# A two-batch encoder layer: all input projections first, in pairs of column tiles with seven products over both batches, and the recurrence after them

## The chip, the cores and the metric

The kernel runs on one core of a Trainium2 chip. The metric is device time of one execution in microseconds: 1835.03 us is the median of two runs (1832.98 to 1837.08). The profiled execution took 1835.74 us. The engines are named as in the profile: PE (TensorE, with PEld for its weight loads), DVE (VectorE), ACT (ScalarE), POOL (GpSimd), SP (SyncE, which issues most transfers).

## What is computed

One layer is applied to two independent requests ("batches") of 512 tokens x 1024 with the same weights. Cut to its core:

```python
h = rmsnorm(x, norm_mix_g)
gates, p_a, pq, pkv, pkr = split(h @ w_in)          # 2048 | 1824 | 256 | 128 | 32 columns
p_a = token_shift(p_a, shift_mu)                    # p + mu0*(previous - p) + mu1*(next - p)
pr, pk, pv, pwf, pwb, paf, pab, pg = split(p_a)     # 3 x 512, 4 x 64, 160
w = exp(-exp(-softplus(-(w0 + tanh(pw) @ w2)) - 0.5))   # decay, forward and backward
a = sigmoid(a0 + pa @ a2);  g = sigmoid(pg) @ g2
# per head of 64, in both directions:
#   S = S*w - (S kk) (kk*a)^T + v k^T ;  o = S r
y_a = ((groupnorm(o_f + o_b) + bonus) * g) @ w_oa
y_b = attention(rmsnorm(pq) @ w_uq, rmsnorm(pkv) @ w_ukv, rope) @ w_ob
x = x + (sigmoid(g_A)*y_a + sigmoid(g_B)*y_b) @ w_out
x = x + (silu(h2 @ w_g) * (h2 @ w_u)) @ w_down ;  out = rmsnorm(x)      # h2 = rmsnorm(x)
```

Everything is float32. Large products are made from operands split into a high and a low part: `mm3` issues three matrix products (high x high, high x low, low x high) that are added in PSUM.

## The kernel before

*Projections.* x is normed and transposed (`norm_T`) into h_hi and h_lo, one pair of tiles per batch. The columns of w_in are cut into 35 tiles of 128. `proj` makes one tile for both batches: 8 steps of 128 rows x 3 products x 2 batches = 48 products of 512 columns (tile 4 in halves of 256). `lora_phase` makes the tiles w, a, g, x and, with `lu` and `lug`, the low-rank products behind them; it ends with the first head pair's r, k and v (`rkv_tiles(0)`). Then `latents` makes the three tiles of q and kv with their norms.

*The recurrence* is made in eight units, one per head pair p and batch b, in the order p outer, b inner. A unit has a preparation (norm of kk with the power on POOL, L714; the gx and gy products; the nt products sent through DRAM as nt_d; on POOL a loop of multiply and subtract over "lanes", L839 and L841, which inverts small triangular blocks), a merge (zp, xp), the state steps (`state`, 8 chunks of three dependent products s with copies between them) and a post part (group norm: mp, ss_gn, rbp_gn, bp) which writes y_d.

*The order of the work.* From the first unit on, `drive` interleaves generators: states, posts, merges and preparations have priority, and fill and combine come last. A planner's clock (`pe["now"]`, advanced by the cost of each product) decides which generator may go on; a yield names how long it is to be left alone. The program order that results is kept on PE (`keep_in_program_order`). The fill is: the other rkv tiles, 16 gate tiles (`gate_tile`), then attention. After the eighth unit `combine` runs per batch: loads of y_d and o_d (`ld`), for each of 8 column tiles j the products pab of both branches, their gates, and the operand m. It is followed by the projection pwo with w_out in quarters of 256 columns, the norm, and the FFN, which already makes its products with seven in place of eight (`gate_up`, `prod`).

*Queues.* SP issues its transfers in the order of its program; a transfer that waits for a semaphore holds those behind it. POOL likewise has one order of lanes, powers and additions.

## Time and profile before

| what | value |
|---|---|
| median of two runs | 1835.03 us |
| profiled execution: time, span | 1835.74 us, 1834.0 us |
| busy PE, DVE, ACT, POOL | 1734.3, 1116.9, 771.0, 642.2 us |
| first projection product, first gx of unit 0 | 27.8, 197.6 us |
| first scores of attention (sc), last state step (s) | 725.8, 898.6 us |
| first pab, first product of the FFN (pgA) | 945.9, 1159.6 us |

A row of the timeline or of the chain gives a start in us, a length and the instruction; x8 means eight of them in a row, and brackets hold the idle time before it with what ended it. A row of a window gives the stretch, its length and, for each engine, the busy time and the number of instructions. A row of groups gives line, engine, operation, out<-in, shapes and count, then busy us and the mean ns of one.

### The profile page before, as it was taken

What the parts mean: (1) busy time and instruction counts of PE and PEld (TensorE: products, weight loads), DVE (VectorE), ACT (ScalarE), POOL (GpSimd) and SP (SyncE); (2) the same over time, 40 slices, a digit from 0 to 9 for tenths busy, and PEclk for the clock granted to TensorE, in tenths of its full rate; (3) what the DMA queues carried; (4) which work ended last, traced back from release to release, by engine and by line L of the source; (5) the groups of instructions that cost most, each with busy time, mean ns of one, the idle gap of its engine ahead of it and who ended that gap; (6) DMA issues with size and microseconds to landing.
All of it is one profiled execution on the core that took longest, in us unless ns stands there. A gap on an engine that the chain in (4) does not pass through costs nothing.

```text
span 1834.0 us, 31000 instructions
## 1 busy us (share of the span) xinstructions
PE 1734.3 (95%) x11676; PEld 1365.7 (74%) x11676; DVE 1116.9 (61%) x1957; ACT 771.0 (42%) x1496; POOL 642.2 (35%) x992
## 2 busy tenths in 40 slices
PE   6999999999999998899989999699999999989997
...
GB/s 163 123 175 163 123 107 82 124 71 136 81 125 106 89 113 119 61 36 55 21 233 249 190 178 35 24 81 93 103 95 84 92 81 92 98 273 134 121 139 92
DMA packets 185333, 208.97 MB, mean 114 GB/s; under 512 B 102816, under 2 KB 114464, under 8 KB 185184
## 3 DMA queue, kind: packets, MB, share of 16 engines
...
q10 hardware_dynamic: 720, 0.98, 0.2%
q0 software_dynamic: 144, 0.52, 0.1%
q14 instruction: 57, 0.47, 0.1%
HBM read 147.70 MB, written 59.24 MB: 113 GB/s over the span
## 4 chain that ended last, share of the span: by engine, by line
PE 70%; DVE 9%; DMA 8%; POOL 5%; issue 3%; ACT 2%; SPq 1%; DVEq 0%; POOLq 0%; ACTq 0%
PE pgC L125 9%; PE pj_gt L125 8%; PE pgB L125 6%; PE pgA L125 6%; PE pj_rkv L125 5%; PE dx L125 5%; PE dy L125 3%; PE s L125 3%; PE pab L125 2%; PE sc L125 2%; PE pav L125 2%; PE pj_mla L125 2%; DMA wor<-in_w_out 2%; PE o L125 2%; PE gx L125 2%
## 5 line engine op out<-in xcount | busy, mean ns | idle before, releaser
L839 POOL TENSOR_TENSOR lt<-lane,el 128x126 f32<-128x126 f32 (+22 forms) x248 | 93.4, 377 | 38.1 <-DMA lane<-nt_d 19.6
L841 POOL TENSOR_TENSOR el<-el,lt 128x126 f32<-128x126 f32 (+22 forms) x248 | 98.6, 398 | 19.0
L125 PE MATMUL pab<-yo,wab 128*128 128x512 f32 x384 | 94.7, 400 | 5.9 <-ACT yo L132 3.2
L125 PE MATMUL pj_gt<-h_hi,whi_gt 128*128 128x512 f32 x240 | 99.2, 413 | 0.0
L125 PE MATMUL pj_gt<-h_hi,wlo_gt 128*128 128x512 f32 x240 | 98.8, 412 | 0.1
L125 PE MATMUL pj_gt<-h_lo,whi_gt 128*128 128x512 f32 x240 | 98.1, 409 | 0.0
L125 PE MATMUL pwo<-woh,m 128*128 128x256 f32 x512 | 93.8, 283 | 0.1
L125 PEld LDWEIGHTS pab<-yo,wab 128*128 128x128 f32 x384 | 71.9, 191 | 26.0 <-DVE wab L133 4.2
L1203 POOL TENSOR_TENSOR s<-uraw 128x512 f32<-128x512 f32 x22 | 29.3, 1330 | 152.1 <-DMA uraw<-in_w_gu 152.1
L125 PEld LDWEIGHTS pwo<-woh,m 128*128 128x128 f32 x512 | 80.3, 192 | 0.6 <-ACT woh L132 0.3
L125 PE MATMUL pj_rkv<-h_hi,wlo_rkv 128*128 128x512 f32 x192 | 79.7, 418 | 0.0
L125 PE MATMUL pj_rkv<-h_lo,whi_rkv 128*128 128x512 f32 x192 | 79.1, 412 | 0.0
L125 PE MATMUL pj_rkv<-h_hi,whi_rkv 128*128 128x512 f32 x192 | 78.3, 408 | 0.0
L125 PE MATMUL pwo<-wol,m 128*128 128x256 f32 x256 | 72.4, 284 | 0.9 <-DVE wol L133 0.9
L1582 POOL TENSOR_TENSOR x<-x,dp 128x512 f32<-128x512 f32 x4 | 6.3, 1590 | 178.1 <-DVE x L1581 178.1
L1271 DVE TENSOR_TENSOR p<-p,pgC 128x512 f32<-128x512 f32 x22 | 15.1, 687 | 86.9 <-PE pgC L125 86.9
L919 ACT COPY sva<-s 64x128 f32<-64x128 f32 x64 | 16.5, 258 | 104.6 <-PE s L125 96.3
L1050 POOL TENSOR_TENSOR g<-g 128x512 f32<-128x512 f32 x16 | 24.9, 1554 | 92.7 <-DVE g L1048 84.5
L466 POOL TENSOR_SCALAR lut<-lut 128x512 f32<-128x512 f32 x32 | 20.5, 641 | 98.4 <-ACT lut L464 98.1
L125 PEld LDWEIGHTS pj_gt<-h_hi,wlo_gt 128*128 128x128 f32 x240 | 45.1, 188 | 9.5 <-DVE wlo_gt L133 0.8
L125 PEld LDWEIGHTS pj_gt<-h_hi,whi_gt 128*128 128x128 f32 x240 | 45.1, 188 | 8.6
L125 PEld LDWEIGHTS pj_gt<-h_lo,whi_gt 128*128 128x128 f32 x240 | 45.1, 188 | 8.4
...
## 6 DMA issues: line engine op xcount, KB each, us to landing
...
```

Source lines behind the costliest of these rows:

```text
L125: pin(nc.tensor.matmul(out, lhsT, rhs, start=start, stop=stop, **kw), n if out.shape[0] > 64 else n / 2)
L466: nc.gpsimd.tensor_scalar(t, t, f, f, op0=ALU.mult, op1=ALU.add)
L839: eng.tensor_mul(lv, lane[:, s, s + 1:].unsqueeze(1).to_broadcast([P, m_, n]), el[:, 0:m_, s].unsqueeze(2).to_broadcast([P, m_, n]))
L841: eng.tensor_add(ev, ev, lv)
L919: nc.scalar.copy(sva[HA, :, c], s2[HA])
L1050: nc.gpsimd.tensor_add(g_[:, 0], g_[:, 0], g_[:, 1])
L1203: vg(ES[min(j, 1)]).tensor_add(s1, a21, a22)
L1271: nc.vector.tensor_add(p1, p1, x_)
L1582: nc.gpsimd.tensor_add(xs(1, t, 1), xs(1, t, 1), p5[t])
```

## The change

Two column tiles and two batches form a 2 x 2 block product over the two halves of the inner dimension. The changed kernel makes it with seven products of blocks in place of eight (`pair`; `single` for the one tile left over). For that the normed x of both batches is kept as the operands H11, H21, H22 (halves of it) and U1 to U4 (their sums and differences over both batches), and each weight block or combination s1 to s4 is made and split when it is needed. A pair is 7 x 4 x 3 = 84 products for what took 96. Seventeen pairs and the single tile make 1476 products of 512 columns, where 35 tiles made 1680.

All pairs now come before the recurrence. The low-rank products and the norms of the latents are queued (`Fill`) between the products of later pairs. Forward and backward low-rank factors now share one weight tile, each in 64 rows, so `lu` issues two products of 64 rows next to each other; the gate's last 32 columns are stacked in 96 rows and take one product in place of three.

The units go batch by batch. The fill beside them is attention, then `branch` of the attention side for either batch, then (after the posts of the first batch's four units) the recurrence side of batch 0, and its projection pwo0 in halves of 512 columns, whose results go through DRAM (x2_d). `tail_thread` waits for all eight posts, loads x, and makes the recurrence side of batch 1. Batch 1's projection stays behind it. In attention the tables carry the negated scale, so the maximum becomes a minimum; the rows are divided after the products with v, with four transposes (`rbp`) per head pair. The copies rs, z and e go from VectorE to ScalarE. `DVE` stands for VectorE in the diff's `nc.vector`, POOL for `nc.gpsimd`.

```diff
-    def proj(ti, name):
...
-                for k in range(KD):
-                    hi, lo = wt[k // 4]
-                    ks = slice(k % 4 * P, (k % 4 + 1) * P)
-                    yield from mm3(res[b][:, qs], hi[:, ks], lo[:, ks], h_hi[b][:, k, qs], h_lo[b][:, k, qs],
-                                   start=(k == 0), stop=(k == KD - 1))
...
+    def prod(ps, wt, op_, first):
+        for k in range(KH):
+            ks = slice(k * P, (k + 1) * P)
+            run(mm3(ps, wt[0][:, ks], wt[1][:, ks], op_[0][:, k], op_[1][:, k],
+                    start=(first and k == 0), stop=False, skip_group_check=True))
...
+    def pair(nm, ta, tb, use, p1=None):
+        ra = w_raw(ta, f"wa{nm}")
+        a11, a12 = ra[:, :512], ra[:, 512:]
+        begun = p1 is not None
+        if not begun:
+            c = abank(0, f"pjA{nm}")
+            prod(c, w_block(a11, f"wA11{nm}"), H11, True)
+            p1 = wp.tile([P, S], F32, tag="p1", bufs=4, name=f"p1w{nm}")
+            nc.scalar.copy(p1, c)
+            yield
+        rb = w_raw(tb, f"wb{nm}")
+        a21, a22 = rb[:, :512], rb[:, 512:]
+        def tmp(i):
+            return wp.tile([P, 512], F32, tag="s", bufs=4, name=f"ws{i}{nm}")
+        s1, s2 = tmp(1), tmp(2)
+        vg(PES[0]).tensor_add(s1, a21, a22)
+        vg(PES[1]).tensor_sub(s2, s1, a11)
+        y = abank(1, f"pjB{nm}")
+        prod(y, w_block(s1, f"wS1{nm}"), U1, True)
+        p5 = wp.tile([P, S], F32, tag="p5", bufs=2, name=f"p5w{nm}")
+        nc.scalar.copy(p5, y)
+        yield
+        e1 = wp.tile([P, S], F32, tag="e1", bufs=2, name=f"e1w{nm}")
+        if begun:
+            s4 = tmp(4)
+            vg(PES[2]).tensor_sub(s4, a12, s2)
+            prod(y, w_block(s4, f"wS4{nm}"), H22, False)
+            nc.vector.tensor_add(e1, y, p1)
+            yield
+        x_ = abank(2, f"pjC{nm}")
+        prod(x_, w_block(s2, f"wS2{nm}"), U2, True)
+        vg(PES[4]).tensor_add(p5, p5, p1)
+        if begun:
+            nc.vector.tensor_add(e1, e1, x_)
+            use(0, 1, e1)
+            yield
+        else:
+            nc.vector.tensor_add(e1, x_, p1)
+            yield
+            prod(c, w_block(a12, f"wA12{nm}"), H21, False)
+            use(0, 0, c)
+            yield
+            s4 = tmp(4)
+            vg(PES[2]).tensor_sub(s4, a12, s2)
+            prod(y, w_block(s4, f"wS4{nm}"), H22, False)
+            nc.vector.tensor_add(e1, e1, y)
+            use(0, 1, e1)
+            yield
+        s3 = tmp(3)
+        vg(PES[3]).tensor_sub(s3, a11, a21)
+        prod(x_, w_block(s3, f"wS3{nm}"), U3, False)
+        nc.vector.tensor_add(p5, p5, x_)
+        use(1, 1, p5)
+        blk = w_block(a22, f"wA22{nm}")
+        yield
+        prod(x_, blk, U4, False)
+        nc.vector.tensor_add(p1, p1, x_)
+        use(1, 0, p1)
...
+        def second(t):
+            ts = slice(t * P, (t + 1) * P)
+            x_norm(4 + t)
+            z0 = x_half(4 + t, 0)
+            nt = np0.tile([P, KH, P], F32, tag="nt", bufs=4, name=f"nt{t}")
+            nc.vector.tensor_sub(nt, z0, H11[0][:, :, ts])
+            nc.vector.tensor_sub(nt, nt, H11[1][:, :, ts])
+            x_split(U1, t, nt)
+            z1 = x_half(4 + t, 1)
+            x_split(H22, t, z1)
+            nc.vector.tensor_sub(nt, z1, nt)
+            nc.gpsimd.tensor_sub(z0, z1, z0)
+            nts.append((nt, z0))
...
+    def products(gen, n):
+        for i in range(n):
+            next(gen, None)
+            fill.step()
+            if i == min(2, n - 1) and late:
+                run(late.pop())
+                fill.step()
+        late.append(gen)
...
+                        ps = [mg(f"lu{b}{p}{e}{d}") for d in range(2)]
+                        for i, j in ((0, 0), (0, 1), (1, 0)):
+                            for d, r in enumerate((slice(0, 64), slice(64, 128))):
+                                mm(ps[d], w2s[e][i][r, sp], lw[e][b][j][r], start=(i == j == 0), stop=(i == 1))
...
+                    run(mm3(ps, g2s[0][:, sp], g2s[1][:, sp], lg[b][0], lg[b][1], stop=False))
+                    mm(ps, g2x[:, sp], lx[b], start=False, stop=True)
...
+    up = lora_wa()
+    rkv_pair(0)
+    fill.q.append(up())
+    rkv_pair(1)
+    gate_pair(4)
+    fill.drain()
+    up = lora_gx()
+    rkv_pair(2)
+    fill.q.append(up())
+    gate_pair(5)
+    fill.drain()
+    norm = latents()
+    rkv_pair(3)
+    fill.q.append(norm())
+    rkv_pair(4)
+    fill.drain()
...
-                mx = ap.tile([P, 4], F32, tag="mx", bufs=4, name=f"mx{b}{hd}{qb}")
-                nc.vector.reduce_max(mx[:, 0:1], sc, axis=AX.X)
-                nc.vector.tensor_scalar_mul(mx[:, 1:2], mx[:, 0:1], -QSCALE)
+                if e == qb == 0:
+                    sums[b, hd // 2] = ap.tile([P, 8], F32, tag="sm", bufs=2, name=f"sm{b}{hd}")
+                sm = sums[b, hd // 2]
+                mx = ap.tile([P, 1], F32, tag="mx", bufs=4, name=f"mx{b}{hd}{qb}")
+                nc.vector.tensor_reduce(mx, sc, axis=AX.X, op=ALU.min)
                 pr = ap.tile([P, S], F32, tag="pr", bufs=ALAG + 1, name=f"pr{b}{hd}{qb}")
-                nc.scalar.activation(pr, sc, AF.Exp, scale=QSCALE, bias=mx[:, 1:2], accum_out=mx[:, 2:3])
-                nc.vector.reciprocal(mx[:, 3:4], mx[:, 2:3])
-                PRE(nc).tensor_scalar(pr, pr, mx[:, 3:4], 0.0, op0=ALU.mult, op1=ALU.add)
+                nc.scalar.activation(pr, sc, AF.Exp, scale=-1.0, bias=mx, accum_out=sm[:, qb * 2 + e:qb * 2 + e + 1])
...
+            ps = pf(f"rbp{b}{p}")
+            tr4(ps, lambda t: rb[:, t * P:(t + 1) * P])
+            nc.scalar.copy(rb, ps)
+            nc.vector.tensor_mul(rb, pav, rb)
+            nc.sync.dma_start(o_d[b][p], rb)
...
-                nc.vector.tensor_copy(rs_, s1)
+                nc.scalar.copy(rs_, s1)
...
-    order = [(b, p) for p in range(NPAIR) for b in range(NB)]
+    order = [(b, p) for b in range(NB) for p in range(NPAIR)]
...
+    def fill_thread():
+        with ExitStack() as sa:
+            yield from attention(pool(sa, "attn", side="right"))
+        mtiles(m0st, 0, side="right")
+        with ExitStack() as s3:
+            ec = pool(s3, "ec", side="right")
+            yield from branch((0,), 1, ec, pf)
+        with ExitStack() as s3:
+            ec = pool(s3, "ec1", side="right")
+            yield from branch((1,), 1, ec, pf)
+        for i in range(NPAIR):
+            yield has("post", i)
+        with ExitStack() as s3:
+            ec = pool(s3, "ec0", side="right")
+            yield from branch((0,), 0, ec, pf, mt[0])
+        wo0["p"] = pool(m0st, "wo0", side="right")
+        for h in range(2):
+            wk = wo_half(0, h)
+            for t in range(4):
+                xq = wo0["p"].tile([P, 512], F32, tag="xq", bufs=2, name=f"xq{h}{t}")
+                nc.sync.dma_start(xq, x[0, t * P:(t + 1) * P, h * 512:(h + 1) * 512])
+                ps = pf(f"pwo0{h}{t}")
+                yield from project(0, wk, t, ps)
+                nc.vector.tensor_add(xq, xq, ps)
+                nc.sync.dma_start(x2_d[t][:, h * 512:(h + 1) * 512], xq)
+        wo0["k"] = wo_half(1, 0)
...
+    def tail_thread():
         for i in range(NU):
             yield has("post", i)
-        yield has("attn", 0)
         rst_.close()
         x2p = pool(p4, "x2p")
         x2.extend(x2p.tile([P, D], F32, name=f"x2_{t}") for t in range(8))
-        for t in range(8):
-            nc.sync.dma_start(x2[t], x[t // 4, (t % 4) * P:(t % 4 + 1) * P, :])
-        mtiles(m0st, 0)
+        for t in range(4):
+            nc.sync.dma_start(x2[4 + t], x[1, t * P:(t + 1) * P, :])
+        fwr.append(pool(ctx, "fwr"))
+        mtiles(sw, 1)
         with ExitStack() as s3:
-            yield from combine(0, pool(s3, "c30"), mg, mt[0])
-    done.add(("rkv", 0))
-    drive([(100000, first_prep()), (0, latents(latp))])
-    slat.close()
+            yield from branch((1,), 0, pool(s3, "c31"), mg, mt[1])
...
+    fill.q.append(first_prep())
+    rkv_pair(5)
+    gate_pair(6)
+    gate_pair(7)
+    flush()
+    fill.drain()
+    hst.close()
     rp = pool(rst_, "rp")
-    drive(list(zip(OFFS, (state_thread(), post_thread(), merge_thread(), prep_thread(), fill_thread(),
-                          combine_thread()))))
+    front = ctx.enter_context(ExitStack())
+    psm.append(ppool(front, "psf"))
+    drive(list(zip(OFFS, (state_thread(), post_thread(), merge_thread(), prep_thread(), tail_thread(),
+                          fill_thread()))))
```

What it does to the order is shown at two places. The first is PE at the end of a unit in the middle: s and o are state products, pj_gt gate projections, mp the post part, ss_kk and rbp_kk the next unit's preparation, pab the output product. Before, at the end of the fifth unit:

```order
L125 MATMUL pj_gt_7060<-h_lo_138,whi_gt_7070 128x512
L125 MATMUL pj_gt_7060<-h_hi_137,wlo_gt_7071 128x512
L125 MATMUL pj_gt_7060<-h_hi_137,whi_gt_7070 128x512
L125 MATMUL pj_gt_7060<-h_lo_138,whi_gt_7070 128x512
L125 MATMUL pj_gt_7060<-h_hi_137,wlo_gt_7071 128x512
L125 MATMUL mp_7101<-os_7090,b_363 128x512
L125 MATMUL ss_kk_7103<-blk2sb,kksq_6996 128x2 x4
L125 MATMUL pj_gt_7060<-h_hi_137,whi_gt_7070 128x512
L125 MATMUL pj_gt_7060<-h_lo_138,whi_gt_7070 128x512
L125 MATMUL pj_gt_7060<-h_hi_137,wlo_gt_7071 128x512
L125 MATMUL pj_gt_7061<-h_hi_139,whi_gt_7064 128x512
```

After, at the end of the same unit:

```order
L126 MATMUL o_8915<-arb_7987,sva_7850 64x64
L126 MATMUL o_8915<-arb_7987,svb_7851 64x64
L126 MATMUL o_8915<-arb_8079,sva_7850 64x64
L126 MATMUL o_8915<-arb_8079,svb_7851 64x64
L126 MATMUL mp_9557<-os_9555,b_3118 128x512
L126 MATMUL ss_kk_9559<-blk2sb,kksq_9510 128x2 x4
L126 MATMUL ss_gn_9567<-blk2sb,osq_9565 128x2 x4
L130 MATMUL rbp_kk_9577<-idn,rb_kk_9575 128x128 x4
L126 MATMUL bp_9586<-bo_9584,b_3118 128x512
L130 MATMUL rbp_gn_9593<-idn,rb_gn_9591 128x128 x4
L126 MATMUL pab_9609<-yo_9379,wab_9603 128x512
```

The products of 512 columns between the state's last o and mp, and between mp and what follows, have gone from this place. Between two successive mp stood 178 products of 512 columns before, up to the fifth. Now attention stands in the first two of these intervals, 96 pab in the third and fourth, 96 pab and 57 pwo in the fifth, 135 pwo in the sixth, and nothing of the kind in the seventh.

The second is SP at the end of the recurrence; x is a tile of the input, wab a weight tile for pab, ld a load of a unit's y_d or o_d, x_d the half results of batch 0. Before:

```order
L957 DMA y_d_114<-os_10247 128x512
L1040 DMA wab_10811<-in_w_oab 128x512
L1040 DMA wab_10882<-in_w_oab 128x512
L1085 DMA x_0_10417<-in_x 128x1024
L1085 DMA x_1_10418<-in_x 128x1024
L1085 DMA x_2_10419<-in_x 128x1024
L1085 DMA x_3_10420<-in_x 128x1024
L1085 DMA x_4_10421<-in_x 128x1024
L1085 DMA x_5_10422<-in_x 128x1024
L1085 DMA x_6_10423<-in_x 128x1024
L1085 DMA x_7_10424<-in_x 128x1024
L567 DMA o_d_104<-ob_10559 128x512
```

After:

```order
L1197 DMA y_d_112<-os_11551 128x512
L1197 DMA y_d_113<-os_11918 128x512
L1262 DMA wab_12009<-in_w_oab 128x512
L1349 DMA x_4_11952<-in_x 128x1024
L1262 DMA wab_12034<-in_w_oab 128x512
L1349 DMA x_5_11953<-in_x 128x1024
L1349 DMA x_6_11954<-in_x 128x1024
L1349 DMA x_7_11955<-in_x 128x1024
L1385 DMA x_0_11948<-x_d_130 128x1024
L1262 DMA wab_12059<-in_w_oab 128x512
L1385 DMA x_1_11949<-x_d_131 128x1024
L1385 DMA x_2_11950<-x_d_132 128x1024
```

The last y_d is now followed by weights, x and the results of batch 0, and the loads of the last batch's y_d stand among and behind these; that of the last y_d is row 472, for its write in row 445. Before, x, loads of o_d and weights follow, and the last y_d is read only after the first batch's products (row 442, for its write in row 354).

672 lines of the change are left out of this document (365 added, 307 removed).

## The prediction

> **What bounds the kernel now.** I read the page first, then a table of windows by stage, then the chain of waits through one unit of the recurrence. The page:
>
> ```profile
> span 1834.0 us, 31000 instructions
> PE 1734.3 (95%) x11676; PEld 1365.7 (74%) x11676; DVE 1116.9 (61%) x1957; ACT 771.0 (42%) x1496; POOL 642.2 (35%) x992
> PE   6999999999999998899989999699999999989997
> ```
>
> TensorE is busy 95% of the span; the digits fall below 9 only in the first slice, at places in the recurrence and attention, in slice 26 (the norm before the FFN) and at the end. The execution took 1835.7 us against a span of 1834.0, so 1.7 lie around it; the median, 1835.0, is the same to 0.7. The stages, with busy time of PE, PEld, DVE, ACT, POOL, then the granted clock, DMA share and GB/s:
>
> ```profile
> 0.00:28.00 28.00, 12.09 (x57) 10.57 (x58) 19.85 (x36) 15.82 (x28) 11.76 (x18) 0.87 0.52 193
> 28.00:198.00 170.00, 167.75 (x799) 138.19 (x801) 81.05 (x131) 75.38 (x122) 34.86 (x57) 0.97 0.43 146
> 198.00:710.00 512.00, 497.32 (x4905) 371.24 (x4901) 261.34 (x524) 194.54 (x409) 252.44 (x576) 0.99 0.38 104
> 710.00:899.00 189.00, 169.22 (x1664) 114.93 (x1664) 143.84 (x361) 115.92 (x270) 66.17 (x145) 0.95 0.21 58
> 899.00:946.00 47.00, 45.07 (x226) 29.15 (x223) 37.71 (x94) 32.15 (x73) 1.64 (x1) 1.00 0.50 183
> 946.00:1107.00 161.00, 152.47 (x845) 127.37 (x844) 96.39 (x159) 56.14 (x99) 35.12 (x23) 0.98 0.59 191
> 1107.00:1160.00 53.00, 50.37 (x417) 49.32 (x416) 35.99 (x58) 21.04 (x38) 27.05 (x24) 1.00 0.10 31
> 1160.00:1834.00 674.00, 640.04 (x2780) 524.89 (x2778) 440.73 (x597) 260.02 (x462) 213.12 (x150) 0.98 0.32 109
> ```
>
> Rows: norm of x; projections up to the first unit; units over rkv and gate products; units over attention; attention alone; output products with the rest of attention; last projection and norm; FFN. A change in products pays where TensorE is the limit, rows 2 and 3. The question is whether row 3 is limited by it alone, for there a unit's own chain runs beneath the fill. The chain through one unit (start, us):
>
> ```profile
> 438.00 1.02 PE gx L125 x16
> 449.24 4.12 DMA nt_d<-nt
> 455.01 3.12 DMA lane<-nt_d
> ...
> 495.08 0.86 PE mp L125 x2
> 495.94 0.79 PE ss_kk L125 x8
> 496.72 3.31 PE pj_gt L125 x14
> 500.82 1.50 PE pj_gt L125 x6
> 502.75 1.62 PE pj_gt L125 x7
> 506.60 1.84 PE pj_gt L125 x8
> 513.41 3.02 PE pj_gt L125 x12
> 517.21 2.26 PE pj_gt L125 x9
> 519.47 1.02 PE gx L125 x16
> ```
>
> POOL between, from its timeline:
>
> ```profile
> 458.29 0.24 POOL L839 TENSOR_TENSOR lt<-lane,el 128x31 f32<-128x31 f32 x1 [3.29 <-DMA lane<-nt_d]
> 490.44 0.23 POOL L841 TENSOR_TENSOR el<-el,lt 128x16 f32<-128x16 f32 x1
> 497.07 1.65 POOL L714 TENSOR_TENSOR rn<-rn,mhalf 128x8 f32<-128x8 f32 x1 [2.00 <-DVE rn L713]
> ```
>
> From one gx to the next, 81.5 us: 20.3 until the first lane operation (458.29 - 438.00), 32.4 of lanes on POOL, 6.4 until the power for the next unit, which is queued on POOL behind the lanes, and 22.4 until the next gx. On this round trip TensorE's fill shows only in the last two parts: 1.50+1.62+1.84+3.02+2.26 = 10.2 us of pj_gt, and the 6.4. So with no fill at all a unit would still need about 81.5 - 10.2 - 6.4 = 65 us. That is a second limit, 20% under the first.
>
> **The change part by part.** The price of a 512-column product, and of vector operations:
>
> ```profile
> 1250.00:1300.00 50.00, 50.00 (x222) 41.40 (x222) 29.86 (x39) 17.01 (x29) 16.16 (x12) 1.00 0.32 111
> L272 DVE TENSOR_SCALAR nh_m<-x,nss_m 128x1024 f32<-128x1024 f32 x8 | 7.9, 984 | 1.5 <-POOL nss_m L172 1.4
> L279 DVE TENSOR_TENSOR nsc_m<-nt_m,col 128x512 f32<-128x512 f32 x10 | 6.7, 680 | 0.0
> L133 DVE TENSOR_TENSOR wlo_w<-wraw_w,whi_w 128x512 fp32r<-128x512 f32 x2 | 3.3, 1712 | 0.0
> ```
>
> 222 in 50 us is 0.225 each, in an FFN stage that makes the same seven products.
>
> *Start.* Before, products begin at 28. Now VectorE has some 87 operations until the operand U1 stands: about 67 x 0.68 + 8 x 0.98 = 53, and 8 until the first data; TensorE has by then only 96 early products and the transposes, 27 us, so 61 when it can run freely. If POOL shares less of VectorE's time than now, 55; with more operations at 1.7, 70.
>
> *Projections.* 17 pairs of 84 and one single of 48 are 1476 products in place of 1680: 204 x 0.225 = 46 us fewer. Behind the first 96: 1380 x 0.225 = 310.5. VectorE does 22 to 25 operations a pair, 15 to 17 us of the 18.9 that a pair takes; where POOL collides (1.7 for one operation) it is the limit. With the statistics and transposes of the latents I add 15; ends 5 and 45.
>
> *Low-rank products.* 96 full ones become 48 pairs of 64 rows, and 48 become 32. No row shows a 64-row product of 512 columns. The nearest are pairs in separate quarters:
>
> ```profile
> 197.28 0.39 PE L125 MATMUL pj_rkv<-h_hi,wlo_rkv 128*128 128x512 f32 x1
> 197.60 0.32 PE L125 MATMUL gx<-kra,bt 64*64 64x128 f32 x1
> 197.61 0.32 PE L125 MATMUL gx<-krb,bt 64*64 64x128 f32 x1
> ```
>
> They start 10 ns apart, so a pair costs one: 48 x 0.225 = 10.8, and 7.2 for the 32; at worst 21.6 and 7.2. Entering this shape took 0.32 - 0.225 = 0.1 us, at 16 groups and two switches 3 us, within the 15 above. The Trainium skill, TensorEngine Tiling (Array Packing), Key Properties, says that tiles of the array run independently but that changing the mode drains it; by it the pairs overlap and the switches cost, and the trace shows both with gx.
>
> *Transition.* first_prep runs beside the last pairs, but gx needs tiles whose memory is freed only after the last product. Of the 22.4 us that prep takes above I take 16.5; ends 5 and 25. First gx: 61 + 310.5 + 15 + 18 + 16.5 = 421 (197.6 before).
>
> *Units.* Their first and last instructions before:
>
> ```profile
> L125 PE MATMUL gx<-kra,bt x256: 269/269/320, 197.6 to 783.3; 64*64 64x128 f32 x128
> L125 PE MATMUL s<-sva,kra x256: 219/222/370, 278.2 to 896.8; 128*64 128x64 f32 x128
> 724.74 0.34 PE L125 MATMUL s<-sva,kra 128*64 128x64 f32 x1 [0.44 <-DVE svb L928]
> ```
>
> Now 699 us from the first gx to the last state step: 80.6 to the first state, seven rounds of 82 (gx: 585.7, less 10 for the last one's own length, by 7), and 45. By the order, 178 products of 512 columns stood between two mp, 40 us; a unit's own TensorE work is then 81.5 - 40 = 41. Now the fill between successive mp is, by the order, attention of 41 and 24 us, 96 pab = 21.6 us twice, 35 and 31 us with pwo, and nothing; a round from state to state takes half of each neighbour. The first two rounds stay at 81 and 82, for VectorE and ScalarE carry attention too (143.8 of 189 in row 4); the third gets 76. Behind it, 41 + 21.6 = 63 is under the 65 of the empty chain, which is not reached either, since pab still stands in front of it: I take 73, 73, 75, then 65, where no further unit is prepared, and 32 for the last state (24 steps at 1.3; the step at 724.74 waits 0.44 behind VectorE). 80.6 + 81 + 82 + 76 + 73 + 73 + 75 + 65 + 32 = 638. TensorE's own sum there is 8 x 41 + attention + 288 pab + 192 pwo, about 565, so 70 us of idle come in, which the fill used to cover. Ends: 590 if the rounds follow TensorE, 700 if they stay.
>
> *Moved copies.* rs, z and e go from VectorE to ScalarE, each on the states' chain with one operation for one: nothing, within the ends above. In attention the row scaling leaves VectorE, and 32 transposes come, 3.5 us of TensorE, inside the 81 and 82.
>
> *Tail.* Before, attention lay between the last state and pab (row 5). Now nothing does: the last y_d is written, and SP then has 9.5 MB ahead of the load of that y_d: eight tiles of x and x2_d at 0.5 MB, three FFN weights at 0.5, four wab, four y tiles and eight of bo_d and rwkv_in at 0.25.
>
> ```profile
> 917.12 0.33 SPq L957 DMA_DIRECT2D y_d<-os  x1
> 920.00:930.00 10.00, 9.61 (x47) 5.80 (x47) 7.89 (x21) 5.43 (x12) 0.00 (x0) 1.00 0.95 356
> L1050 POOL TENSOR_TENSOR g<-g 128x512 f32<-128x512 f32 x16 | 24.9, 1554 | 92.7 <-DVE g L1048 84.5
> ```
>
> At 356 GB/s, the full queues' rate, 9.5 MB are 27 us; with the last group norm, 10, and the split of y, 2, it is 39 from the last state to pab. Before, y_d went out at 917.1, 20 behind the last state (896.8), beneath attention. Ends 20 (loads of x overtake) and 55. Then 96 pab, 22 by products, 30 as each j waits for gate, POOL's 1.55 and two buffers; then the last projection as in row 7, 51 for 53. Sum 120, for 261 before, as attention and three quarters of the output products have moved. pwo in 512 columns is counted in the units. The clock is at stake wherever TensorE waits; the norm stage shows it:
>
> ```profile
> 1150.00:1200.00 50.00, 32.92 (x156) 25.75 (x155) 46.48 (x44) 18.39 (x33) 40.02 (x26) 0.83 0.07 21
> ```
>
> The Trainium skill, TensorE: Matmul & The Clock Gate, Part 1, says the clock halves after an idle window of about 3.4 us and returns after as much busy time. The 0.83 agrees. An estimate by it is 2 us more behind the tail's wait.
>
> *FFN.* Unchanged products: 674.
>
> Sum: 421 + 638 + 120 + 674 + 1.7 = **1855 us**, 1% above 1835.7: 46 + 14 + 9 us of products are gone, and about 90 of waiting come in.
>
> **Rivals.** *TensorE stays the limit everywhere.* Speaking for it: 95% busy, and the planner fills gaps it foresees. 1834 - 46 - 11 - 4 (low rank) - 6 (pwo: 768 of half width to 384) + 3.5 + 1.7 = 1772. Against: 63 under 65 in the middle units, and no work beside the last. *The units do not shorten* (slower): the round trip's lanes, DMAs and power are kept as they are, and the 16.6 us of fill in it are replaced by the waits they covered. Then 7 x 82 + 80.6 + 45 = 700 in place of 638: 1917. It decides if the fill-short rounds measure over 79. For: the lanes and DMAs fill 53 of 81.5, whatever TensorE does. Against: pj_gt stands on the chain in its own name. *The pairs are limited by VectorE, or the low-rank pairs do not overlap*: 2 us a pair and 11, some 30 to 40: 1890.
>
> **How the numbers follow.** A measurement here can tell about 2%, so faster is below 1798 and slower above 1872. My forecast gets 0.47 (0.36 within 2%, 0.11 above, its own range 1815 to 1890 by the ends of tail, transition and units), TensorE everywhere 0.24 (0.22 faster, 0.02 within), units not shorter 0.15 (slower), the pairs' limit 0.14 (0.10 slower, 0.04 within). That makes 0.22, 0.42 and 0.36. The range 1778 to 1908 leaves out half of the first rival and the upper part of the second.
>
> **What would show it.** First gx near 421 and nearly full TensorE until then but for the first 61 us; rounds from state to state of 73 to 76 from the third unit on, with TensorE waiting for DVE, POOL and lane loads; some 29 us without TensorE between the last bp and pab, ended by ld<-y_d; FFN 674. If first gx comes before 400, or TensorE is over 95% busy in the middle rounds, or pab starts within 20 us of the last state, the forecast is too high; if the rounds stay at 82, too low.

## The result and the profile after

The changed kernel takes 1990.02 us (median of two runs, 1988.41 to 1991.63) against 1835.03: a ratio of 1.0845, with an interval of 1.078 to 1.0909. It is 8% slower; the prediction was 1855, and its range ended at 1908. The page of the kernel after:

```profile
span 1989.8 us, 30003 instructions
PE 1733.7 (87%) x11056; PEld 1340.7 (67%) x11056; DVE 1183.5 (59%) x1852; ACT 864.9 (43%) x1714; POOL 707.9 (36%) x1032
PE   6699999979989987886889747669999999989998
PEclk9899999989999997787998657799999999999999
```

TensorE's busy time is the same to 0.6 us (1734.3 before) with 620 matrix instructions fewer, since in several slices its clock is lower (last row); the span has grown by 155.8, as much as the time in which TensorE stands. Behind the first two slices the digits fall below 9 at places from slice 9 to 27, where the units and the tail lie. The same execution by stage, with the columns of the prediction's windows (PE, PEld, DVE, ACT, POOL, clock, DMA share, GB/s):

```profile
28.00:70.00 42.00, 24.04 (x104) 18.42 (x105) 42.00 (x50) 17.06 (x31) 20.00 (x13) 0.81 0.32 93
70.00:426.00 356.00, 350.58 (x1584) 280.58 (x1582) 230.10 (x347) 169.53 (x286) 80.75 (x83) 0.99 0.38 128
426.00:446.70 20.70, 9.54 (x23) 5.82 (x22) 13.08 (x23) 11.43 (x23) 1.65 (x6) 0.67 0.52 160
...
525.30:624.00 98.70, 85.00 (x854) 58.30 (x853) 56.31 (x108) 61.02 (x145) 41.45 (x92) 0.95 0.23 59
...
708.10:791.40 83.30, 67.26 (x727) 49.66 (x726) 41.57 (x81) 38.83 (x89) 40.82 (x92) 0.80 0.42 116
791.40:872.80 81.40, 66.67 (x715) 48.94 (x714) 41.71 (x79) 33.36 (x75) 41.66 (x92) 0.81 0.49 140
872.80:966.80 94.00, 68.78 (x716) 50.57 (x715) 47.98 (x85) 34.21 (x76) 51.76 (x96) 0.80 0.50 148
966.80:1069.00 102.20, 86.50 (x802) 62.04 (x801) 54.12 (x98) 40.98 (x88) 52.62 (x98) 0.92 0.49 143
1069.00:1135.50 66.50, 54.84 (x658) 40.20 (x657) 25.40 (x54) 22.88 (x60) 36.50 (x81) 0.80 0.30 78
1135.50:1166.10 30.60, 23.42 (x305) 18.84 (x304) 6.10 (x21) 4.25 (x16) 4.76 (x12) 0.50 0.01 2
1166.10:1205.60 39.50, 10.08 (x30) 5.36 (x28) 6.30 (x10) 5.37 (x9) 4.16 (x3) 0.50 0.66 247
...
1238.90:1312.90 74.00, 54.80 (x248) 44.33 (x248) 35.70 (x52) 21.10 (x37) 27.14 (x24) 0.86 0.10 35
1312.90:1989.80 676.90, 641.70 (x2781) 523.75 (x2779) 441.64 (x596) 260.58 (x463) 209.91 (x149) 0.98 0.32 108
```

Two rows of the kernel before, its rounds (from one unit's first state step to the next unit's) at the same places as 83.3 and 81.4 above:

```profile
439.30:520.70 81.40, 78.28 (x800) 57.96 (x799) 38.29 (x81) 30.67 (x65) 39.45 (x92) 1.00 0.38 103
520.70:599.00 78.30, 77.69 (x800) 57.94 (x799) 39.33 (x82) 31.75 (x67) 39.67 (x92) 1.00 0.38 104
```

Before, TensorE was busy for 78 of such a round; now for 67, and the round is no shorter. That is the case in two rows. The stages in us ("first state" is from the first gx to the first state step):

| | before | predicted | after |
|---|---|---|---|
| start to first gx | 197.6 | 421 | 446.7 |
| first state | 80.6 | 80.6 | 78.6 |
| seven rounds | 80.8 80.3 81.4 78.3 78.8 97.2 78.6 | 81 82 76 73 73 75 65 | 98.7 84.1 83.3 81.4 94.0 102.2 66.5 |
| last state | 45.2 | 32 | 30.6 |
| last state to FFN | 260.8 | 120 | 146.8 |
| FFN to end | 674.4 | 674 | 676.9 |

Between the two kernels the head has grown by 249.1, the units by 18.2 and the FFN by 2.5, and the tail (last state to FFN) has shrunk by 114.0. Before, most projections and gate tiles were made inside rounds that would have lasted nearly as long without them (g1, below). Taken out of there they cost their full time ahead, and the rounds kept theirs.

### The profile page after: what moved, and what is told of

Its sections match the earlier page's. It is cut to its first block, busy times and chain, and to the rows that moved or that the text cites. A ratio compares the mean times of both kernels' runs of the same rounds, so it can differ in the third digit from the quotient of the medians.

```text
span 1989.8 us, 30003 instructions
## 1 busy us (share of the span) xinstructions
PE 1733.7 (87%) x11056; PEld 1340.7 (67%) x11056; DVE 1183.5 (59%) x1852; ACT 864.9 (43%) x1714; POOL 707.9 (36%) x1032
## 3 DMA queue, kind: packets, MB, share of 16 engines
q1 hardware_dynamic: 181808, 217.54, 34.3%
## 5 line engine op out<-in xcount | busy, mean ns | idle before, releaser
L126 PE MATMUL pwo<-woh,m 128*128 128x512 f32 x256 | 90.6, 422 | 5.9 <-ACT woh L133 5.9
L126 PEld LDWEIGHTS pwo<-woh,m 128*128 128x128 f32 x256 | 50.1, 199 | 17.8 <-ACT woh L133 7.2
L848 DVE TENSOR_REDUCE mx<-sc 128x1 f32<-128x512 f32 x64 | 43.6, 684 | 27.4 <-PE sc L126 26.6
L1135 ACT COPY rs<-s 128x128 f32<-128x128 f32 x64 | 17.0, 265 | 97.3 <-PE s L126 94.8
L126 PE MATMUL s<-sva,bka 128*64 128x64 f32 x224 | 28.2, 257 | 34.5 <-DVE svb L1160 34.2
L126 PE MATMUL pwo<-wol,m 128*128 128x512 f32 x128 | 54.2, 424 | 2.8 <-DVE wol L134 2.8
L126 PE MATMUL sc<-kt,qh 128*128 128x512 f32 x128 | 51.8, 476 | 3.8 <-ACT qh L133 3.0
L1457 POOL TENSOR_TENSOR s<-graw,uraw 128x512 f32<-128x512 f32 x22 | 29.2, 1327 | 62.9 <-DVE S_2l L134 5.9
L850 ACT ACTIVATE pr<-sc,mx 128x512 f32<-128x512 f32 x64 | 44.1, 689 | 14.8 <-DVE mx L848 13.4
L130 PE MATMUL pt<-idn,pr 128*128 128x128 f32 x256 | 40.3, 282 | 10.8 <-ACT pT L788 7.8
L126 PE MATMUL s<-rs,e 64*64 64x64 f32 x512 | 32.3, 253 | 16.4 <-ACT rs L1135 16.1
L130 PEld LDWEIGHTS pt<-idn,pr 128*128 128x128 f32 x256 | 31.4, 144 | 21.1 <-ACT pT L788 10.0
```

The costliest lines, as they stand in the source:

```text
L126: pin(nc.tensor.matmul(out, lhsT, rhs, start=start, stop=stop, **kw), n if out.shape[0] > 64 else n / 2)
L130: pin(nc.tensor.transpose(ps[:, t * P:(t + 1) * P], src(t), idn), P / 1200)
L848: nc.vector.tensor_reduce(mx, sc, axis=AX.X, op=ALU.min)
L850: nc.scalar.activation(pr, sc, AF.Exp, scale=-1.0, bias=mx, accum_out=sm[:, qb * 2 + e:qb * 2 + e + 1])
L1135: nc.scalar.copy(rs_, s1)
L1457: vg(ES[min(j, 1)]).tensor_sub(s3, a11, a21)
```

## The experiments

Stage times in us of every run, in the order of the rows above. An interval is that of the ratio to the kernel before (its time between 1835.7 and 1839.5 beside these runs); totals without one are single runs. The tail ends at the first product of the FFN (pgA). e1, e11, e13, e15, f1, f3 and g1 leave work out that the layer needs.

| run | total | first gx | first state | rounds | last state | tail |
|---|---|---|---|---|---|---|
| after | 1990.0 [1.078, 1.0909] | 446.7 | 78.6 | 98.7 84.1 83.3 81.4 94.0 102.2 66.5 | 30.6 | 146.8 |
| e1 | 1922.0 | 449.5 | 79.1 | 103.2 84.5 76.3 78.1 73.0 73.5 60.2 | 30.4 | 134.4 |
| g1 (of before) | 1854.7 | 196.8 | 77.3 | 79.9 84.8 75.7 76.3 75.8 92.9 79.9 | 47.3 | |
| e15 | 1912.2 | 457.0 | 78.6 | 82.1 75.6 75.8 82.4 76.2 74.4 65.5 | 30.3 | 134.0 |
| e13 | 1920.6 | 445.5 | 85.6 | 95.1 92.0 73.3 83.6 69.2 67.4 68.2 | 29.1 | 131.9 |
| e2 | 2019.6 | 448.1 | 78.2 | 104.3 84.3 80.5 72.7 89.3 91.3 93.9 | 46.7 | 151.1 |
| e7 | 2004.8 [1.0894, 1.0943] | 446.5 | 86.6 | 88.5 87.7 79.0 79.1 84.6 103.4 79.6 | 40.7 | 150.2 |
| e6 | 2036.3 | 446.3 | 78.3 | 82.8 89.0 91.8 84.9 86.8 86.0 100.6 | 52.0 | 157.3 |
| e3 | 1976.1 | 458.8 | 78.2 | 82.1 75.7 75.4 84.5 83.7 109.6 69.4 | 34.3 | 145.8 |
| f1 | 1961.9 | 448.4 | 78.2 | 97.1 84.1 82.4 83.0 88.6 79.4 62.9 | 30.3 | 145.7 |
| e11 | 1982.2 | 447.9 | 78.5 | 98.0 84.3 84.1 82.3 91.8 91.9 64.5 | 30.4 | 146.3 |
| f2 | 1977.9 | 446.4 | 78.0 | 97.1 83.8 81.9 82.1 89.2 103.2 65.9 | 30.3 | 140.5 |
| f3 | 1977.8 | 448.3 | 78.2 | 96.5 84.0 81.4 82.5 86.5 99.4 66.5 | 30.4 | 146.2 |
| e8 | 1992.0 [1.0827, 1.0871] | 449.4 | 79.8 | 100.9 84.5 82.6 82.4 91.9 101.8 66.6 | 30.6 | 143.3 |
| e14 | 1985.4 [1.0772, 1.0835] | 449.1 | 78.2 | 104.4 84.0 83.8 83.9 89.1 101.7 66.9 | 30.6 | 136.6 |
| e9 | 1993.4 [1.0838, 1.0884] | 447.3 | 80.2 | 97.3 83.1 85.2 82.3 92.9 103.6 66.0 | 30.5 | 145.4 |
| e10 | 1974.8 [1.0738, 1.0770] | 459.2 | 77.8 | 82.8 76.2 77.4 82.6 82.2 112.4 69.9 | 34.2 | 141.4 |

### How long is a round with nothing beside it? (e1, g1, e15)

The prediction said 65. e1 takes the fill behind attention out of the kernel after:

```diff
-        mtiles(m0st, 0, side="right")
-        with ExitStack() as s3:
-            ec = pool(s3, "ec", side="right")
-            yield from branch((0,), 1, ec, pf)
...
-            yield from branch((0,), 0, ec, pf, mt[0])
...
-            wk = wo_half(0, h)
...
-                yield from project(0, wk, t, ps)
-                nc.vector.tensor_add(xq, xq, ps)
```

> Left out: all output products beside the units (both attention sides, batch 0's recurrence side, pwo0), with their loads, gates and splits; the units, attention and batch 1's tail stay. Theory 1 (a round is a chain of VectorE, POOL and DMA work of about 80 us that the fill never lengthened; the gate products in the chain of waits stood beside it): rounds from state to state from the third on stay at 78 to 82, only the sixth and seventh (94 and 102 us now) fall to about 80, total 1945 to 1960. Theory 2 (the empty chain is 65 us as predicted, and pab's loads, splits and gates on the other engines take the gain away): rounds of 65 to 70, total about 1890.

Its fifth and sixth rounds, by windows:

```profile
870.70:943.70 73.00, 47.00 (x624) 36.35 (x623) 28.82 (x62) 26.24 (x63) 38.32 (x93) 0.67 0.24 61
943.70:1017.20 73.50, 51.57 (x622) 39.72 (x621) 28.86 (x63) 26.19 (x63) 38.35 (x91) 0.61 0.23 57
```

The bare rounds, those with nothing beside the units (third to sixth), last 73 to 78. That lies between the two expectations, 78 to 82 and 65 to 70. The units are 61 us shorter than after's, and still 20 longer than predicted with all fill in them.

g1 asks the same of the kernel before, on whose chain the 65 were read. Its gate products are replaced by a constant, and attention is held back:

```diff
-                yield from gate_tile(j, e)
+                for b in range(NB):
+                    t = sh(f"gtt{j}{e}{b}")
+                    nc.gpsimd.memset(t, 0.5)
+                    nc.sync.dma_start(gate_d[b][j][:, e], t)
+        yield has("state", 5)
```

> The kernel before, with the fill taken from its middle rounds: the products of the gate tiles are left out (the gate is a constant written by POOL), and attention waits until the state of unit 5 is done, so that rounds 3 to 5 run with nothing but the units' own work. Its output is not the reference's. My theory (the 65 us of the prediction were read wrongly: the rows of pj_gt on the chain of waits stood beside the unit's own VectorE preparation, lane loads and waits) expects bare rounds of 73 to 78 us here too, as in the bare kernel after. The prediction's reading (pj_gt and the wait for the power can be taken out of 81.5) expects 65 or 66. A third way, that 73 to 78 comes only from something in the kernel after (copies on ScalarE, other places of the loads), would also give 65 here.

Three of its rounds have no fill at all (75.7, 76.3 and 75.8). Two of them:

```profile
438.80:514.50 75.70, 48.29 (x624) 37.21 (x623) 32.51 (x74) 22.66 (x51) 38.38 (x93) 0.64 0.23 58
514.50:590.80 76.30, 48.34 (x622) 37.17 (x621) 32.53 (x75) 22.66 (x51) 38.73 (x93) 0.65 0.23 58
```

178 products a round are gone and TensorE stands for 27 of 76 us, yet the rounds are only 2 to 6 us under the full ones of the same units (81.4, 78.3, 78.8). From the gx at 511.0 to that at 586.7 the same four pieces as in the prediction are 17.6 to the first lane, 32.5 of lanes, 4.5 until the power, 21.2 until gx: 75.8 where it had 20.3 + 32.4 + 6.4 + 22.4 = 81.5. So taking the fill away is worth 5.7, and only 3.1 of it comes from the last two pieces, from which the prediction took 16.6. What fills these two pieces is in g1's timeline, by PE, DVE and POOL:

```profile
562.09 1.86 PE L125 MATMUL ss_kk<-blk2sb,kksq 128*128 128x2 f32 x8
563.99 0.17 DVE L713 TENSOR_SCALAR rn<-ss_kk 128x8 f32<-128x8 f32 x1 [2.57 <-PE ss_kk L125]
564.57 0.53 POOL L825 MEMSET el<- 128x512 f32 x1 [2.03 <-DMA e_d<-el]
565.51 1.65 POOL L714 TENSOR_TENSOR rn<-rn,mhalf 128x8 f32<-128x8 f32 x1
572.64 1.22 DVE L734 TENSOR_TENSOR_SCAN c<-rst,c 128x512 f32<-128x512 f32 x1 [0.62 <-DMA c<-rwkv_in]
580.28 1.23 DVE L734 TENSOR_TENSOR_SCAN c<-rst,c 128x512 f32<-128x512 f32 x1 [0.81 <-DMA c<-rwkv_in]
585.30 1.43 PE L125 MATMUL xp<-e,z 32*32 32x32 f32 x32 [3.63 <-DVE e L879]
```

The power waits for ss_kk, which stands on TensorE behind the state's last o, and on POOL behind an el that waits for the transfer e_d: neither is fill. Then VectorE prepares the unit, with two scans that each wait for a load. The same stretch, from the power to gx, in g1, in before and in after, one row each:

```profile
565.50:586.70 21.20, 11.14 (x149) 7.88 (x148) 14.51 (x24) 8.87 (x14) 5.36 (x7) 0.50 0.36 103
```

```profile
497.10:519.50 22.40, 22.27 (x217) 16.72 (x217) 15.73 (x26) 11.29 (x19) 6.19 (x9) 1.00 0.53 157
```

```profile
765.20:789.00 23.80, 19.66 (x190) 14.54 (x190) 16.29 (x26) 12.53 (x22) 6.66 (x12) 0.82 0.59 177
```

VectorE is busy for 14.5 to 16.3 us of 21 to 24 in all three. In the kernel before TensorE was full beside it (22.27 of 22.40), so the chain of waits, followed back from gx, ran along TensorE's own rows and named pj_gt.

These bare rounds of g1 were granted a clock of 0.64 to 0.65, where the full rounds had 1.00. Does the slow clock make 76 out of 65? TensorE's rows on g1's chain of waits, from gx to gx, are:

```profile
510.98 3.25 PE gx L125 x32
531.68 0.70 PE s L125 x8
532.37 0.62 PE o L125 x8
533.00 1.04 PE tk L129 x4
534.04 0.65 PE s L125 x8
585.67 1.06 PE xp L125 x30
```

They are 7.3 of 75.8 us (7.8 and 8.8 in the other two bare rounds). POOL has 24, transfers 22 and VectorE 11. The lowest clock in the rows is 0.50, so a full clock would take off at most half of TensorE's part, about 4 us, and leave 71 or more; this is an estimate from these rows.

e15 adds to e1 that the power is taken out of the unit (the edit of e3, below):

> As the run without fill, and with the kk norms of all units made ahead of the units. If the power behind the lanes is a link of the chain whether or not there is fill, the bare rounds fall from 73-78 to 65-70, as the first three fell by 17, 8 and 8 with fill, and the total to 1870 to 1890. If it only mattered in front of the fill, they stay within 3 us.

This shortens the first two rounds (82.1 and 75.6 for 103.2 and 84.5), where attention still runs, and none of the bare ones. So the 6.4 of the power were not to be had either.

### Is it the clock, or the order? (e13, e2, e7, e6)

Bare rounds are granted 0.61 to 0.78 of the clock, and after's rounds 3 to 5 are granted 0.80. Their waits are short. The three longest on TensorE from 715 to 800 of after, with line, releaser, total, times and longest:

```profile
PE rbp_kk L130 <- ACT rb_kk L186: 4.4, 1, 4.4
PE s L126 <- ACT rs L1135: 4.3, 2, 2.2
PE s L126 <- DVE svb L1160: 3.3, 3, 1.4
```

The mean of 0.80 is, in each of rounds 3 and 4, mainly one stretch at half the clock:

```profile
739.80:770.50 30.70, 20.40 (x153) 16.08 (x152) 9.97 (x22) 11.64 (x28) 22.14 (x50) 0.50 0.30 80
825.10:855.80 30.70, 20.44 (x138) 14.92 (x136) 9.99 (x21) 11.19 (x28) 19.58 (x45) 0.50 0.31 85
```

It begins behind five us in which TensorE was busy for only 1.5 (735 to 740) and 2.2 (820 to 825); from 715 to 735 the clock is 1.00. TensorE is busy for 20.4 us in either stretch. At the full clock that would be 10 less, so a round could gain 10 at most, and only if all of this work lay on the chain (an estimate from these rows; the chain of waits of this run does not reach back to these rounds). The Trainium skill, TensorE: Matmul & The Clock Gate, A second HAM failure mode: psum-queue depth-cycling, says that short idle times between groups of products can be frequent enough to make the clock go back and forth. These two rounds do not show that: the clock falls and stays low for 31 us.

Useless products were added in four runs. e7 has a generator of lowest priority, 612 products in all; e13 has nearly the same (624) beside e1's bare units; e2 makes each pab beside the units twice; e6 puts 24 products of zeros in each unit behind the state's steps.

```diff
+    def filler():
+        dmy = rp.tile([P, P], mybir.dt.bfloat16, name="dmy")
+        nc.gpsimd.memset(dmy, 0.7)
+        while ("post", NU - 1) not in done:
+            ps = pf("fl")
+            for i in range(12):
+                pin(nc.tensor.matmul(ps..., dmy, ..., start=(i == 0), stop=(i == 12 - 1)), S / 2400)
+                yield 0
```

> A further generator of lowest priority puts 612 useless products of 512 columns (0.22 us each at full clock, 135 us of TensorE) into the gaps that the planner sees beside the units; nothing reads them. If the clock that falls to 0.8 in these rounds is what lengthens them (with twice the pab the fourth round took 72.7 us at 0.99, for 81.4 at 0.81), the rounds from the third on fall to 72 to 78 at a clock over 0.95, and the total is no longer than 1990, perhaps 1960, for all the added work. If TensorE's work or its in-order queue sets the rounds, the total grows by 60 to 135 us.

> As the run without fill (no output products beside the units), with about 600 useless products of 0.22 us spread over the units, which wait for nothing and which nothing reads. Without them the bare rounds took 73 to 78 us at a granted clock of 0.61 to 0.78. If a slow clock is what separates these from the forecast 65, they fall to 64 to 69 at a clock over 0.95, and the total falls below the 1922 of the run without fill, to about 1900, although TensorE does 135 us more. If the clock is off the chain, they stay at 73 to 78 or grow.

```diff
-                for k in range(NPAIR):
+                for k in list(range(NPAIR)) * (2 if newps is pf else 1):
```

> Every pab product beside the units is made twice (the second pass starts its sum anew): 288 products, 65 us of TensorE more, no other work. Theory 1 (the rounds are a chain beside TensorE): most of it is hidden in TensorE's idle time and the clock rises from 0.8, total at most 25 us longer. Rival (the rounds follow TensorE, through its in-order queue or its work): total 50 to 65 us longer.

```diff
                 last = c == NCH - 1
+                for _ in range(1):
+                    mm(op..., zr, ..., start=False, stop=False, skip_group_check=True)
                 yield L1
...
```

> Each step of the states gets one more product of zeros of 512 columns that adds nothing to o: 24 in a unit, 5 us of TensorE, put where it waits for the copies. If the low granted clock (0.79 to 0.81 in the rounds with 96 pab) is what keeps these rounds at 83, the clock rises to 0.95 or more and they fall to about 73. If the clock is only a sign of waiting, rounds change by less than 3 us either way.

Rounds 5 and 6 of e13, and round 4 of e2:

```profile
875.10:944.30 69.20, 59.48 (x723) 35.86 (x722) 28.75 (x61) 26.68 (x63) 39.54 (x92) 0.95 0.25 64
944.30:1011.70 67.40, 59.21 (x723) 35.78 (x722) 28.42 (x60) 25.81 (x63) 38.58 (x89) 0.95 0.25 62
```

```profile
795.40:868.10 72.70, 67.90 (x746) 50.10 (x745) 31.11 (x64) 26.14 (x63) 38.85 (x87) 0.99 0.39 105
```

With more products, e2's round 4 takes 72.7 where after takes 81.4, and e13's 69.2 and 67.4 where e1 takes 73.0 and 73.5; the clock is 0.95 to 0.99 there. But rounds 3 to 7 of e13 sum to 361.7 against 361.1 of e1, since rounds 4 and 7 grew by 5.5 and 8.0; and e13 as a whole takes 1920.6 against 1922.0, with some 135 us of products more. In e7 rounds 3 and 4 were granted 1.00 and took 79.0 and 79.1, where 72 to 78 had been expected. The added 135 us cost 15 there, and in e2 65 us cost 30. So work beside the units costs none to half of itself: that is shown, in single runs but for e7.

That the clock at 0.80 makes rounds 3 and 4 longer by some 5 us fits e2, e7 and two rounds of e13, but the added products move the order too. From gx to gx, the chains through e1's rounds 5 and 6 hold 3.0 and 5.6 us of TensorE and 20 and 18 of transfers; those of e13, 5.5 and 5.7 us shorter, hold 11 and 12 of transfers. Half of e1's TensorE part is 1.5 and 2.8, so by these rows the clock alone gives at most half of what was gained; the rest goes with the order, by which less of transfers lies on the chain. What the clock costs with pab beside the units stays open. e6 came out slower by 46 for 42 us added, on the states' path, at a clock of 0.81 to 0.92, and decides nothing.

### The first round (e3)

After's first round is 98.7 against 80.8 before. In its timeline, behind lanes that end at 580.9:

```profile
581.44 3.65 PE L126 MATMUL pav<-pT,vt 128*64 128x512 f32 x14
585.02 1.12 PE L126 MATMUL mp<-os,b 128*128 128x512 f32 x2
593.45 1.03 PE L126 MATMUL ss_kk<-blk2sb,kksq 128*128 128x2 f32 x8
593.94 1.66 POOL L172 TENSOR_TENSOR gnr<-gnr,mhalf 128x8 f32<-128x8 f32 x1 [7.03 <-DVE gnr L171]
595.57 1.64 POOL L954 TENSOR_TENSOR rn<-rn,mhalf 128x8 f32<-128x8 f32 x1
```

The next unit's norm stands behind attention and mp, and its power ends 16.4 behind the lanes, where it was 8.7 at the same place before. e3 makes the norms of all units between the last projections:

```diff
+        def norm(self):
...
+            kk = tmp("kn")
+            nc.sync.dma_start(kk, rwkv_in[b][p][:, 1])
+            nc.scalar.activation(kk, kk, AF.Square, scale=cc(C_KK + p))
...
+            ss = row_stats(_MG(), kk, 2, f"kk{nm}")
+            self.rn = rp0.tile([P, 8], F32, name=f"rn{nm}")
...
-            ss = row_stats(_MG(), sq, 2, f"kk{nm}")
...
-            nc.gpsimd.tensor_tensor(rn, rn, mhalf[:, :8], op=ALU.pow)
+            rn = self.rn
```

> The row norms of kk of all eight units, with their power on POOL, are made between the last two pairs, so that no power stands behind the lanes of the unit before. If the link lanes, power, next gx sets the round (as the prediction had it), rounds fall by the 6 us between lanes and power and by part of the wait behind it: 6 to 15 us each, total 1880 to 1940. If the round is set by two units in turn (state, then the next but one unit's preparation, lanes, merge, state), rounds fall by less than 4 us and the total by less than 25.

Round 1 falls to 82.1, round 2 to 75.7, round 3 to 75.4; 12 us come back in the first gx and 7 in round 6: 14 us in all. So the late norm and power made the first round long, by some 17 us, and rounds 2 and 3 by 8; behind these three rounds, and in the bare rounds of e15, their place was worth nothing.

### Rounds 5 and 6 (f1, e11, f2, f3)

They take 196.2 where 148 was predicted. f1 leaves pwo0 out (weights, products, additions), e11 keeps it and loads and splits one weight block in place of eight, f2 moves the additions on loaded y tiles and of the two gated branches from POOL to VectorE, f3 reads o_d in place of y_d for batch 0, with four loads in place of twelve and no additions ahead of the products; it waits for the posts all the same.

```diff
-            wk = wo_half(0, h)
...
-                yield from project(0, wk, t, ps)
-                nc.vector.tensor_add(xq, xq, ps)
```

> Left out: batch 0's projection beside the units, with its weights (its x goes on unchanged). Batch 0's recurrence side stays. If the projection and its weights are what makes rounds five and six 196 us together where the forecast had 148 (without any fill 146), they fall to 160 or less; if it is the recurrence side with its loads of y and its additions, they stay over 180.

```diff
-        for k in range(KD):
+        for k in range(KD if b else 1):
...
-        return wk
+        return wk * (KD // len(wk))
```

> For batch 0's projection beside the units only one of the eight row blocks of each half of w_out is loaded and split, and is used for all eight (the output of batch 0 is then not the reference's): the 192 products stay, seven of eight weight loads, casts and splits go. If the sixth round (102 us, for 75 forecast) is long because casts and splits that wait for these weights stand in ScalarE's and VectorE's queues ahead of the states' copies, it falls to 80 to 88. If it is TensorE's work of 135 products, or the additions on POOL, it stays over 95.

```diff
-            nc.gpsimd.tensor_add(t, t, bg[:, 0])
+            nc.vector.tensor_add(t, t, bg[:, 0])
...
-                nc.gpsimd.tensor_add(g_[:, 0], g_[:, 0], g_[:, 1])
+                nc.vector.tensor_add(g_[:, 0], g_[:, 0], g_[:, 1])
```

> The additions of bo_d to y and of the two gated branches go from POOL to VectorE, nothing else. If additions that wait for loads hold up the lanes queued behind them on POOL (45 and 39 us of lanes in units five and six for 33), rounds five and six fall by 12 to 20 us together; if other waits end as late, they stay within 5 of 196.

```diff
-        nc.sync.dma_start(t, (y_d, o_d)[e][b][p])
-        if e == 0:
+        nc.sync.dma_start(t, (y_d, o_d)[1 if b == 0 else e][b][p])
+        if e == 0 and b:
```

> Batch 0's recurrence side reads the attention side's results again in place of y_d, bo_d and the gate (its output is then not the reference's): the same 96 products, splits and gates, but four loads that are ready long before in place of twelve, and no additions ahead of it. If loads of results just written are what stops the queues in round five (94 us, TensorE busy 3.8 of the 10 us from 915), it falls to 80 to 84; if the splits and products cost it, it stays over 90.

Rounds 5 and 6 sum to 168.0, 183.7, 192.4 and 185.9. So pwo0 holds 28, of which its weights (transfers, casts, subtractions) hold about 12; the loads of y and what is added to it hold 10; POOL's additions 4 (f2's total falls by 12, 6 of it in the tail). f1, e11 and f3 came out between their two expectations. The four are single runs, and the parts overlap: e11's 12 lie within f1's 28. What is left of the 48 was not separated further.

### The tail (e8, e14)

The last y_d is written at 1179.1 and read at 1203.2; the products with it come after 1208. On SP, PE and ScalarE:

```profile
1179.05 0.34 SPq L1197 DMA_DIRECT2D y_d<-os  x1
1203.20 0.32 SPq L1243 DMA_DIRECT2D ld<-y_d  x1
...
1200.12 0.80 PE L126 MATMUL pab<-yo,wab 128*128 128x512 f32 x1 [22.74 <-ACT yo L133]
...
1257.66 0.62 ACT L133 CAST woh<-wor 128x512 fp32r<-128x512 f32 x1 [0.94 <-DMA wor<-in_w_out]
1258.19 1.06 ACT L1406 ACTIVATE nhf<-x 128x1024 f32<-128x1024 f32 x1
```

The first pab starts 34 behind the last state, as the forecast of 39 had it, for loads that stand in SP's order behind x and weights: with x loaded later (e8) it is 26. The last two rows show what it didn't have: the first norm's square (nhf) needs no weight and stands on ScalarE behind eight casts of weights that wait for their loads. The four norms then follow one another at 6 to 8 us, and the FFN starts at 1312.9. e8 writes the norms ahead of pwo1 in the program and the loads of x behind the branch; e14 gives the branch four buffers in place of two, and has the later loads too.

```diff
-        for t in range(4):
-            nc.sync.dma_start(x2[4 + t], x[1, t * P:(t + 1) * P, :])
         fwr.append(pool(ctx, "fwr"))
...
             yield from branch((1,), 0, pool(s3, "c31"), mg, mt[1])
+        for t in range(4):
+            nc.sync.dma_start(x2[4 + t], x[1, t * P:(t + 1) * P, :])
...
     for t in range(4):
+        first_norm(t)
+    for t in range(4):
         ps = dn(f"pwo1{t}0")
...
-        first_norm(t)
```

> Behind the units alone: the four norms of batch 0 are put ahead of batch 1's first half projection in the program, and batch 1's x is loaded after the recurrence side's own loads. If the 76 us from the last pab to the FFN are the norms' chain standing behind weight splits on ScalarE, this stretch falls to about 52; if the 39 us ahead of pab are the queue of loads on SP, it falls to about 30. Together the total falls by 25 to 35 us, to about 1958. If the norms' chain is exposed wherever it stands, or the loads of y_d are late for their own latency, it falls by under 10.

```diff
+        nb = 4 if newps is mg else 2
...
-                split(yo[b][0][:, p], yo[b][1][:, p], y_ld(cp_, b, e, p))
+                split(yo[b][0][:, p], yo[b][1][:, p], y_ld(cp_, b, e, p, nb))
...
-                g_ = cp_.tile([P, 2, S], F32, tag="g3", bufs=2, name=f"g3{j}{b}{e}")
+                g_ = cp_.tile([P, 2, S], F32, tag="g3", bufs=nb, name=f"g3{j}{b}{e}")
```

> In the tail alone, batch 1's y loads and their bo_d and rwkv_in rows get four buffers instead of two, and so do its gates; batch 1's x is loaded after them. If the two buffers, which are free again only after POOL and VectorE, are what puts the last y at 40 us behind the last state, pab starts 8 to 12 us earlier and the 33 us of pab fall to 26: total about 1973. If it is the amount of data on the queues (9.5 MB at 250 to 350 GB/s), pab starts as now, total 1985 to 1995.

e8 leaves the total as it was. The first pab comes 8 us nearer, but the pab then take 44.1 us for 38.6, and ScalarE's order of casts and norm stayed the same. e14 takes 10 us off the tail; on the total, 1985.4 against 1990.0, the intervals overlap. A version with the norms truly ahead of the casts was not tried, so what their place costs is not shown.

### The moved copies (e9), and the best together (e10)

```diff
-                nc.scalar.copy(rs_, s1)
+                nc.vector.tensor_copy(rs_, s1)
...
-                    nc.scalar.copy(z_[...], zp[...])
+                    (nc.scalar.copy, nc.vector.tensor_copy)[h](z_[...], zp[...])
```

> The copies rs, z and e are given back to VectorE as they were. The forecast put the move at nothing: total within 6 us of 1990. If ScalarE, busy with attention's exponentials and the splits of weights, held the states' steps up, the first rounds (98.7 and 84.1) and the third and fourth fall by 3 us or more each and the total by 15 to 40.

No effect can be measured: 1993.4 against 1990.0, with intervals that overlap. e10 has the edits of e3, e8 and f2 together, and loads the identity first:

```diff
+    nc.sync.dma_start(idn, ident)
...
-            if i == 3:
-                nc.sync.dma_start(idn, ident)
```

> Together: the kk norms of all units ahead of the units, batch 0's recurrence additions on VectorE instead of POOL, the identity loaded ahead of x, and the two edits of the tail. By single effects: 14 us from the norms, 10 to 25 from lanes that no longer share POOL with waiting additions (45 and 39 us of lanes in units 5 and 6 for 33), up to 8 at the start, 30 in the tail: total 1910 to 1935. If the chain finds another holder for each, 1945 to 1965. Either way over the 1835 of the kernel before.

1974.8 is the best of the versions that compute everything, but only 1.3 us under e3 alone, and over both ranges that had been expected of it: round 6 grew to 112.4 while 1 to 3 shrank. None of the versions of the kernel after comes near the kernel before; even e15, which leaves a large part out, takes 4% more.

## Why the prediction was wrong, and where it was right

The sum was 137 us short of the span: 26 in the head, 81 in the units, 27 in the tail, 3 in the FFN.

- *The empty chain of 65, the step that failed.* "So with no fill at all a unit would still need about 81.5 - 10.2 - 6.4 = 65 us." Without fill the kernel before needs 76 (g1; 71 or more at a full clock, by the estimate above) and the kernel after 73 to 78 (e1). The pj_gt on the chain of waits stood beside VectorE's preparation and its loads, and the power waits for the norm of kk, not for fill. The two 73s, the 75 and the 76 rested on it. The prediction put 8 on the empty chain for pab in front of it, 65 + 8 = 73; 76 + 8 is 84, and rounds 3 and 4 measured 83.3 and 81.4. With 11 more in each of the four rounds 3 to 6 the forecast would have had 341 us for them, where it had 297 and 361 were measured: 44 of the 81. Rounds 5 and 6 (196 against 148) have the waits of pwo0, of y and of POOL besides, which the 8 did not hold; that is the other 20.
- *The rival "the units do not shorten"* had the mechanism, at 0.15: the removed fill "replaced by the waits they covered". Its test, fill-short rounds over 79, was met (83.3, 81.4); its 700 for the units were 719. The argument against it, that pj_gt is on the chain in its own name, was the error.
- *"The first two rounds stay at 81 and 82."* 98.7 and 84.1. VectorE and ScalarE do carry attention (61 of ScalarE's 98.7), but it was the kk norm's place behind attention that cost 17 in the first, as e3 shows.
- *Last round and last state.* 66.5 and 30.6 for 65 and 32: right. The round that came out at 65 is the one that no further preparation follows, and says nothing of the others.
- *First gx.* Each term came out over its middle value: start 70 for 61, products, low rank and norms 356 for 343.5, transition 20.7 for 16.5. At the start VectorE is busy in all 42 us of the first row, and products wait for U1:

```profile
63.05 0.80 PE L126 MATMUL pjBg<-U,wS1g0h 128*128 128x512 f32 x1 [10.57 <-ACT U L133]
69.36 0.80 PE L126 MATMUL pjBg<-U,wS1g0h 128*128 128x512 f32 x1 [5.09 <-DVE U L134]
```

- *Low-rank pairs.* They overlap. All lu products in one window:

```profile
70.00:420.00 350.00, 15.46 (x96) 7.92 (x96) 20.26 (x32) 0.99 0.39 129
```

96 products of 64 rows took 15.5 us, as 48 pairs 0.32 each; the forecast was 10.8 and 3 for switches, and 21.6 without overlap. What the Trainium skill, TensorEngine Tiling (Array Packing), Key Properties, says of tiles that run independently agrees with it. VectorE does not limit the pairs: 230 of 356, while TensorE has 351.
- *Tail.* 34 to pab for 39, right in size, and 8 of it are loads of x by e8; pab 39 for 30; the last projection and norm 74 for 51. The 51 was taken from a row of before; that the norms stand behind casts now is seen, that this makes the 23 is not shown.
- *Clock.* "2 us more" was far too little as a view of it: the last state ran at 0.50, the tail up to pab at 0.50, three rounds at 0.80. What that cost in the rounds with fill stays open (above).
- *FFN 674, moved copies nothing:* 677, and no effect that can be measured.
- *A count that doesn't fit.* The account behind the sum has 9 us of pwo's products gone, the sum of the first rival 6; the 1855 uses neither.
